# Stick-breaking mask added on VectorE instead of two GpSimd selects, first loads from two queues, and a planned order with margins for waits

## The chip, the core and the metric

The kernel runs on one core of a Trainium2 chip. A core has five engines that run side by side and meet through semaphores: TensorE (PE in the profile, with its weight loads as PEld), VectorE (DVE), ScalarE (ACT), GpSimd (POOL) and SyncE (SP), which here does nothing but issue DMAs. Each engine takes its instructions strictly in the order of its own queue; an instruction that has to wait holds up everything behind it. The metric is the device time of one launch in microseconds (us), the median of three runs.

## The reference

One decoder layer over 512 tokens and a width of 1024, all in fp32. The normalised input is multiplied by one wide input matrix, its columns feed four groups of four heads (64 wide) that mix in four ways, and every group's output is gated, concatenated and multiplied by the output matrix.

```python
def hybrid_layer(x, norm_gain, w_in, b_forget, fox_qk_gain, moba_qk_gain, swa_qk_gain, sinks, w_out, rel_bias):
    hn = rms_norm(x, norm_gain)
    proj = jnp.einsum('btd,de->bte', hn, w_in)
    (fq, fk, fv, ff, fg, mq, mk, mv, mg, sq, sk, sv, sg, wq, wk, wv, wg) = split_columns(proj)
...
    y = jnp.concatenate([from_heads(o_fox) * jax.nn.silu(fg),
                         from_heads(o_moba) * jax.nn.silu(mg),
                         from_heads(o_sb) * jax.nn.silu(sg),
                         from_heads(o_swa) * jax.nn.silu(wg)], axis=-1)
    return x + jnp.einsum('bte,ed->btd', y, w_out)
```

The change touches the arithmetic of one group alone, the stick-breaking heads, called `s` in the kernel (the others are `f`, `m` and `w`):

```python
        z = jnp.einsum('bhqd,bhkd->bhqk', q_i, k).astype(jnp.float32) * ATTN_SCALE
        strict = pos[None, :] < t[:, None]
        log_keep = jnp.where(strict, jax.nn.log_sigmoid(-z), 0.0)
        suffix = lax.cumsum(log_keep, axis=3, reverse=True) - log_keep
        a = jnp.where(strict, jnp.exp(jax.nn.log_sigmoid(z) + suffix), 0.0)
        return jnp.einsum('bhqk,bhkd->bhqd', a.astype(v.dtype), v)
```

The kernel reverses the token order on the host, so that a query block sees itself and the blocks behind it, and the reversed sum over keys becomes a running sum from the left.

## The kernel before

Every fp32 operand of a large product is split into a high part (written by ACT, `hi_copy`, line 134) and a low part (the difference, written by DVE in `lo_part`, lines 139 to 142, or for weight chunks named in `POOL_LO` by GpSimd at line 250). A product is then three matmuls, high by high, high by low, low by high (`mm3`, lines 336 to 338). A 512-wide one starts about 0.23 us after the one before.

Weights come in chunks of up to 512 KB into three raw buffers (`raw`, filled by `load_raw`, line 214), in the order `sv`, `sqk`, `fvf`, `fqk`, `fg`, `sg`, `mqk`, `mv`, `mg`, `wg`, `wqkv`, `o`. A chunk is split into `wh` and `wl`; its raw buffer is then free for the chunk three places later.

The program begins with matmuls of zeros (`warm`, line 156), then loads x transposed (`xT`, eight slices), the first weights (`sv`, two chunks of four loads each) and the small vectors in the order of the string `LOADS` (lines 263 to 272), all of them from SP. ACT loads its table first (line 145). x in its natural layout comes in eight loads (line 769) in the order of `NORMS`; `x_norm` (line 295) makes of two of them the factors `rx` of 128 tokens. When all four are there, `r_row` (line 318) transposes them on PE (tile `rT`), copies them out (`rt`) and sends them through DRAM to all partitions (`rrow`). Line 778 multiplies the `sqk` projections with `rrow`, from which queries and keys of the `s` heads are split (`qs_s`, `k`).

A stick-breaking head (`sb_head`, line 560) does four blocks i of 128 queries against 512, 384, 256 and 128 keys. Per block: scores on PE (lines 505 and 506, or 501 for the last block, tile `s_s`, two PSUM banks in turn), three functions on ACT (lines 577 to 579), a maximum and a sum on DVE (580), a select on GpSimd that zeroes the masked corner (581), the running sum on DVE (583), a difference on DVE (584), a second select on GpSimd that puts -1e30 into the corner (585) and an exponential on ACT (587). The results are transposed on PE (`pT_s`, line 518), copied out in two parts (`pth`, `ptl`) and multiplied with the values (`o_s`, lines 468 and 469). In a tile's name s_s23 is head 2, block 3.

Attention of one group runs among the projections of the next: after each projection step `attend` (line 784) lets the heads go forward by `RATE` units, and by `OUTU` units beside the first half of the output product. The written order is not the final one: `order_engines` (line 1097) reads all instructions, and `_plan` (line 1028) simulates them with costs and latencies written in the program and gives every engine a fixed order. `TURN` moves groups of instructions forward or back in priority, and `PATIENCE` lets an engine wait a little for one of higher priority.

## Time and profile before

| what | value |
|---|---|
| median of 3 runs | 295.74 us (294.53 to 296.07) |
| the profiled execution | 296.93 us |
| its span, first to last instruction | 295.2 us |
| DVE busy | 220.4 us (75%) |
| ACT busy | 194.6 us (66%) |
| GpSimd busy | 116.1 us (39%) |
| bytes moved by DMA | 33.65 MB, mean 114 GB/s |
| granted TensorE clock, mean | 0.994 |

Busy time is the union of an engine's instructions. Matmuls overlap in the array, and their ends are modelled, so an idle stretch of PE in the profile is really idle, while a pause of some 0.1 us between two matmuls does not show. "PEclk" is the TensorE clock that was granted, as a share of full speed. In a row of the timeline stand start, duration, engine, line, operation, tiles and shapes, and in brackets the idle time before it with the one that ended it.

### The profile page before, as it was taken

How to read it: one execution, taken by the hardware profiler on the slowest of the kernel's cores; microseconds unless marked ns; L12 is line 12 of the kernel's file. 1: busy time of each engine (PE TensorE's matmuls, PEld its weight loads, DVE VectorE, ACT ScalarE, POOL GpSimd, SP SyncE). 2: the span in 40 equal slices, each digit the busy share in tenths (PEclk: the TensorE clock that was granted, in tenths of full speed). 3: DMA queues.
4: the chain of work that ended last, by engine and by line, in shares of the span. 5: the costliest groups of instructions: out<-in, count | busy, mean ns of one | idle time of the engine just before them, and what ended most of it. 6: DMA issues, size and time to landing. Idle time of an engine off the chain costs nothing.

```text
span 295.2 us, 4695 instructions
## 1 busy us (share of the span) xinstructions
PE 283.5 (96%) x1529; PEld 236.0 (80%) x1529; DVE 220.4 (75%) x584; ACT 194.6 (66%) x445; POOL 116.1 (39%) x194
## 2 busy tenths in 40 slices
PE   8998999999997899999997999999999999999995
PEld 8987889888885688877876997788888868888884
DVE  1868287969889873699999626896579668999353
ACT  4866089986798653398784447966897839676200
POOL 4505204854157784566426022203440698001010
PEclk9999999999999799999999999999999999999999
DMA  6993606060134059731205412331400345400024
GB/s 194 342 394 124 197 3 188 26 205 18 64 80 136 1 180 263 188 121 37 45 29 149 137 50 92 110 107 30 132 1 18 107 146 192 163 3 0 2 107 178
DMA packets 19960, 33.65 MB, mean 114 GB/s; under 512 B 1616, under 2 KB 10068, under 8 KB 19808
## 3 DMA queue, kind: packets, MB, share of 16 engines
q1 hardware_dynamic: 19936, 33.35, 36.2%
q8 instruction: 12, 0.20, 0.3%
q14 instruction: 12, 0.10, 0.1%
HBM read 31.22 MB, written 4.22 MB: 120 GB/s over the span
## 4 chain that ended last, share of the span: by engine, by line
PE 64%; DVE 13%; ACT 11%; DMA 8%; issue 2%; SPq 1%; POOL 1%; POOLq 0%; DVEq 0%; ACTq 0%
PE o L338 4%; PE o L337 4%; PE o L336 4%; DMA xT<-in_xT 3%; DMA raw_sqk<-in_w_in 3%; PE p_wqkv L336 3%; PE p_wqkv L337 3%; PE p_wqkv L338 3%; PE p_sqk L336 2%; PE p_sqk L338 2%; PE p_sqk L337 2%; ACT k L134 2%; PE pT_m L518 1%; PE pT_f L518 1%; DMA fbc<-sd 1%
## 5 line engine op out<-in xcount | busy, mean ns | idle before, releaser
L250 POOL TENSOR_TENSOR wl_wqkv<-raw_wqkv,wh_wqkv 128x260 fp32r<-128x260 f32 (+1 forms) x12 | 8.5, 737 | 35.9 <-ACT wh_wqkv L134 35.9
L250 POOL TENSOR_TENSOR wl_fqk<-raw_fqk,wh_fqk 128x260 fp32r<-128x260 f32 (+1 forms) x12 | 9.6, 817 | 14.8 <-PE s_s L506 14.1
L583 DVE TENSOR_TENSOR_SCAN pm_s<-l 128x512 f32<-128x512 f32 (+3 forms) x16 | 14.3, 891 | 0.5 <-POOL l L581 0.5
L250 POOL TENSOR_TENSOR wl_o<-raw_o,wh_o 128x260 fp32r<-128x260 f32 (+1 forms) x12 | 9.0, 780 | 14.3 <-issue 14.3
L487 POOL TENSOR_TENSOR oc_w<-oc_w,gate_w 128x512 f32<-128x512 f32 x2 | 2.6, 1285 | 28.3 <-DVE oc_w L482 28.3
L336 PE MATMUL p_sqk<-xh,wh_sqk 128*128 128x512 f32 x32 | 12.6, 400 | 1.0 <-ACT wh_sqk L134 1.0
L585 POOL TENSOR_SCALAR_AFFINE_SELECT pm_s<-pm_s 128x128 f32<-128x128 f32 x16 | 8.9, 556 | 11.2 <-DVE pm_s L584 9.3
L669 POOL TENSOR_SCALAR fxb<-fbc,scol 128x512 f32<-128x512 f32 (+3 forms) x16 | 9.1, 572 | 10.5 <-DMA fbc<-sd 5.2
L336 PE MATMUL p_mqk<-wh_mqk,xh 128*128 128x512 f32 x32 | 13.1, 408 | 0.0
L338 PE MATMUL p_mqk<-wh_mqk,xl 128*128 128x512 f32 x32 | 12.9, 402 | 0.0
L336 PE MATMUL p_wqkv<-wh_wqkv,xh 128*128 128x512 f32 x32 | 12.9, 402 | 0.0
L337 PE MATMUL p_wqkv<-wl_wqkv,xh 128*128 128x512 f32 x32 | 12.8, 401 | 0.0
L336 PE MATMUL p_fqk<-wh_fqk,xh 128*128 128x512 f32 x32 | 12.8, 405 | 0.0
L337 PE MATMUL p_mqk<-wl_mqk,xh 128*128 128x512 f32 x32 | 12.8, 399 | 0.0
L337 PE MATMUL p_fqk<-wl_fqk,xh 128*128 128x512 f32 x32 | 12.8, 399 | 0.0
L338 PE MATMUL p_fqk<-wh_fqk,xl 128*128 128x512 f32 x32 | 12.7, 397 | 0.0
L338 PE MATMUL p_wqkv<-wh_wqkv,xl 128*128 128x512 f32 x32 | 12.6, 395 | 0.0
L139 DVE TENSOR_TENSOR ptl_s<-pT_s,pth_s 128x384 fp32r<-128x384 f32 (+3 forms) x16 | 7.4, 484 | 6.7 <-ACT pth_s L134 6.7
L337 PE MATMUL p_sqk<-xl,wh_sqk 128*128 128x512 f32 x32 | 12.3, 391 | 0.0
L338 PE MATMUL p_sqk<-xh,wl_sqk 128*128 128x512 f32 x32 | 11.7, 390 | 0.0
L581 POOL TENSOR_SCALAR_AFFINE_SELECT l<-l 128x128 f32<-128x128 f32 x16 | 6.9, 433 | 11.5 <-DVE l L580 10.1
L518 PE MATMUL pT_s<-ident,pm_s 128*128 128x128 f32 x40 | 7.9, 279 | 2.9 <-ACT pm_s L587 2.8
(353 smaller groups left out, 1134.6 us busy)
## 6 DMA issues: line engine op xcount, KB each, us to landing
raw_o<-in_w_out SPq DMA_DIRECT2D x8, 512.0 KB, 3.3
xT<-in_xT SPq DMA_DIRECT2D x8, 256.0 KB, 4.1
raw_sqk<-in_w_in SPq DMA_DIRECT2D x4, 512.0 KB, 6.9
x<-in_x SPq DMA_DIRECT2D x8, 256.0 KB, 7.2
raw_fqk<-in_w_in SPq DMA_DIRECT2D x4, 512.0 KB, 3.7
raw_mqk<-in_w_in SPq DMA_DIRECT2D x4, 512.0 KB, 3.7
raw_wqkv<-in_w_in SPq DMA_DIRECT2D x4, 512.0 KB, 3.5
xr<-in_x SPq DMA_DIRECT2D x4, 512.0 KB, 3.5
```

The costliest lines, as they stand in the source:

```text
L134: nc.scalar.activation(dst, src, AF.Copy if isinstance(scale, float) else AF.Identity, scale=scale)
L139: nc.vector.tensor_tensor(dst, src, hi.bitcast(F32), op=ALU.subtract)
L250: nc.gpsimd.tensor_tensor(lv[q], rv[q], hv[q].bitcast(F32), op=ALU.subtract)
L336: nc.tensor.matmul(dst, ah, bh, start=first, stop=False)
L337: nc.tensor.matmul(dst, ah, bl, start=False, stop=False)
L338: nc.tensor.matmul(dst, al, bh, start=False, stop=last)
L487: nc.gpsimd.tensor_tensor(oc, oc, gates[e], op=ALU.mult)
L518: nc.tensor.transpose(pt[:, a * P:(a + 1) * P], pm[:, o:o + P], ident)
L581: nc.gpsimd.affine_select(l[:, :P], l[:, :P], pattern=[[1, P]], base=-1, channel_multiplier=-1, compare_op=ALU.is_ge, fill=0.0)
L583: nc.vector.tensor_tensor_scan(seg, l, l, 0.0, ALU.add, ALU.bypass)
L585: nc.gpsimd.affine_select(seg[:, :P], seg[:, :P], pattern=[[1, P]], base=-1, channel_multiplier=-1, compare_op=ALU.is_ge, fill=NEG)
L669: nc.gpsimd.tensor_scalar(b, bc[:, i * P:], -1.0, scol[:, i, h:h + 1], op0=ALU.mult, op1=ALU.add)
```

## The change

The two GpSimd selects of each stick-breaking block go. In their place a 128x128 tile `smask` (zero, and -1e30 where masked) is made once, and DVE adds it to the masked corner of the scores before ACT reads them, in PSUM in place (for the last block of a head in SBUF). The three functions and the maximum then give zero there by themselves.

The first three loads of `sv` are issued by ACT, ahead of its table load, and `LOADS` has another order. The natural x of tokens 256 to 511 (`HELD`, loads 4 to 7) is planned behind the weight load last issued. Six chunks leave `POOL_LO` (20, 27, 28, 30, 33, 35: one of `mqk`, three of `wqkv`, two of `o`), so that DVE makes their low parts. `RATE` and `OUTU` are smaller, `TURN` has other numbers, and the planner counts a DMA slower and 500 ns later and adds a margin to each wait of PE and ACT on another engine.

```diff
-LOADS = "w0 x0 s x1 w1 x2 w2 x3 w4 w3 x4 x5 w5 x6 w6 w7 x7 q"
-NORMS = "a 0 1 2 3 4 5 6 7 a a a a"
+LOADS = "w0 x0 w1 s w2 x1 x2 x3 w3 x4 w4 x5 w5 x6 w6 x7 w7 q"
+NORMS = "a 0 1 2 3 4 5 a 6 7 a a a"
+BY_ACT, HELD = "w0 w1 w2", {4, 5, 6, 7}
-RATE, OUTU = 5.5, 1.6
+RATE, OUTU = 4.54, 0.55
-POOL_LO = {1, 4, 6, 9, 10, 12, 15, 16, 17, 19, 20, 21, 23, 24, 27, 28, 30, 33, 34, 35, 36, 37,
-           38}
+POOL_LO = {1, 4, 6, 9, 10, 12, 15, 16, 17, 19, 21, 23, 24, 34, 36, 37, 38}
...
-PATIENCE = {"Pool": 10}
+PATIENCE = {"Pool": 10, "PE": 54}
+MARGIN = {"PE": 100, "Activation": 41}
...
-            first[k // 4][k % 4]()
+            first[k // 4][k % 4](nc.scalar if n in BY_ACT.split() else nc.sync)
...
+        if n == BY_ACT.split()[-1]:
+            nc.scalar.preload_act_table_set("natural_log_exp_and_others")
...
+    smask = sb.tile([P, 512], F32, tag="band", name="smask", bufs=2)[:, :P]
+    nc.gpsimd.memset(smask, 0.0)
+    nc.gpsimd.affine_select(smask, smask, pattern=[[1, P]], base=-1, channel_multiplier=-1,
+                            compare_op=ALU.is_ge, fill=NEG)
...
+            nc.vector.tensor_tensor(z[:, :P], z[:, :P], smask, op=ALU.add)
+
             nc.scalar.activation(l, z, AF.Abs)
             nc.scalar.activation(l, l, AF.Exp, scale=-1.0)
             nc.scalar.activation(l, l, AF.Ln, bias=one)
             nc.vector.scalar_tensor_tensor(l, z, 0.0, l, op0=ALU.max, op1=ALU.add)
-            nc.gpsimd.affine_select(l[:, :P], l[:, :P], pattern=[[1, P]], base=-1,
-                                    channel_multiplier=-1, compare_op=ALU.is_ge, fill=0.0)
             nc.vector.tensor_tensor_scan(seg, l, l, 0.0, ALU.add, ALU.bypass)
             nc.vector.tensor_tensor(seg, z, seg, op=ALU.subtract)
-            nc.gpsimd.affine_select(seg[:, :P], seg[:, :P], pattern=[[1, P]], base=-1,
-                                    channel_multiplier=-1, compare_op=ALU.is_ge, fill=NEG)
             nc.scalar.activation(seg, seg, AF.Exp)
...
-            nc.sync.dma_start(xn[t][h], x[t * P:(t + 1) * P, h * 512:(h + 1) * 512])
+            with behind_loads() if int(n) in HELD else nullcontext():
+                nc.sync.dma_start(xn[t][h], x[t * P:(t + 1) * P, h * 512:(h + 1) * 512])
...
-                queue = max(t + 1130, queue) + big * 4 / 360.0
+                queue = max(t + 1130, queue) + big * 4 / 335.0
                 rings.append(queue)
-            src, end = "DMA", queue
+            src, end = "DMA", queue + 500
...
+                if wait and src != e:
+                    d += margin.get(e, 0)
```

The start on ScalarE, before: its first six instructions, where raw_sv is a first weight, wh_sv its high part, xT a slice of x transposed and xh its scaled high part.

```order
L145 ACT_TABLE_LOAD
L134 ACTIVATE wh_sv0_155<-raw_sv0_108 128x256
L134 ACTIVATE xh0_131<-xT0_92,small_70 128x512
L134 ACTIVATE xh0_131<-xT1_93,small_70 128x512
L134 ACTIVATE wh_sv0_155<-raw_sv0_108 128x256
L134 ACTIVATE xh0_131<-xT2_94,small_70 128x512
```

ScalarE at the start, after the change.

```order
L216 DMA raw_sv0_107<-in_w_in 128x256 x3
L276 ACT_TABLE_LOAD
L137 ACTIVATE wh_sv0_160<-raw_sv0_107 128x256 x2
L137 ACTIVATE xh0_131<-xT0_91,small_69 128x512
L137 ACTIVATE wh_sv0_160<-raw_sv0_107 128x256
L137 ACTIVATE xh0_131<-xT1_92,small_69 128x512
L137 ACTIVATE xh0_131<-xT2_93,small_69 128x512
```

Three weight loads now stand ahead of the table load, and two weight splits ahead of the first slice of x.

SyncE's queue from the first `sqk` chunk on, before: x00 to x31 are the eight loads of natural x, two for each 128 tokens.

```order
L214 DMA raw_sqk0_110<-in_w_in 128x2x512
L769 DMA x00_100<-in_x 128x512
L769 DMA x01_101<-in_x 128x512
L769 DMA x10_102<-in_x 128x512
L769 DMA x11_103<-in_x 128x512
L769 DMA x20_104<-in_x 128x512
L769 DMA x21_105<-in_x 128x512
L214 DMA raw_sqk1_221<-in_w_in 128x2x512
L769 DMA x30_106<-in_x 128x512
L769 DMA x31_107<-in_x 128x512
L214 DMA raw_sqk2_289<-in_w_in 128x2x512
L214 DMA raw_sqk3_367<-in_w_in 128x2x512
```

SyncE at the same place, after the change.

```order
L216 DMA raw_sqk0_109<-in_w_in 128x2x512
L777 DMA x00_99<-in_x 128x512
L777 DMA x01_100<-in_x 128x512
L777 DMA x10_101<-in_x 128x512
L777 DMA x11_102<-in_x 128x512
L216 DMA raw_sqk1_226<-in_w_in 128x2x512
L216 DMA raw_sqk2_294<-in_w_in 128x2x512
L777 DMA x20_103<-in_x 128x512
L777 DMA x21_104<-in_x 128x512
L216 DMA raw_sqk3_354<-in_w_in 128x2x512
L777 DMA x30_105<-in_x 128x512
L777 DMA x31_106<-in_x 128x512
```

The second and third `sqk` chunk moved ahead of x20, and the last loads of x behind all four chunks.

PE before, around the last transposition of head 2 (pT_s23; its input pm_s2 is the last of the rows of s_s23): p_fg1 is the second projection step of a gate. From s_s23 to this row stand 12 projection matmuls.

```order
L337 MATMUL p_fg1_1377<-xl0_133,wh_fg0_798 128x512
L338 MATMUL p_fg1_1377<-xh0_131,wl_fg0_799 128x512
L336 MATMUL p_fg1_1377<-xh0_131,wh_fg0_798 128x512
L337 MATMUL p_fg1_1377<-xl0_133,wh_fg0_798 128x512
L518 MATMUL pT_s23_1105<-ident_83,pm_s2_1003 128x128
L338 MATMUL p_fg1_1377<-xh0_131,wl_fg0_799 128x512
```

PE at the same transposition, after the change; p_sg0 is the first step of the next gate.

```order
L342 MATMUL p_sg0_1364<-xh0_131,wl_sg0_1083 128x512
L340 MATMUL p_sg0_1364<-xh0_131,wh_sg0_1082 128x512
L341 MATMUL p_sg0_1364<-xl0_133,wh_sg0_1082 128x512
L522 MATMUL pT_s23_1147<-ident_82,pm_s2_1024 128x128
L342 MATMUL p_sg0_1364<-xh0_131,wl_sg0_1083 128x512
L340 MATMUL p_sg0_1364<-xh0_131,wh_sg0_1082 128x512
```

The transposition stands later by 28 projection matmuls: from s_s23 to it there are now 40 (8 of fg0, 24 of fg1, 8 of sg0).

DVE before, the rows that end with the difference of block s_s23 (l_23 is its work tile, ruf and r0f belong to a query norm).

```order
L741 TENSOR_TENSOR gate_f0_1342<-p_fg0_1317,rrow_135 128x512
L368 TENSOR_REDUCE qms_f3_1196<-sq_f3_1194 128x8
L282 SCALAR_TENSOR_TENSOR ruf2_1081<-r0f2_1079 128x8
L580 SCALAR_TENSOR_TENSOR l_23_1091<-l_23_1091 128x128
L139 TENSOR_TENSOR ptl_s22_1119<-pT_s22_1114,pth_s22_1118 128x384
L283 TENSOR_TENSOR ruf2_1081<-ruf2_1081,rmf2_1080 128x8
L279 TENSOR_SCALAR rmf3_1199<-qms_f3_1196,ex_130 128x8
L583 SCALAR_TENSOR_TENSOR pm_s2_1003<-l_23_1091 128x128
L287 SCALAR_TENSOR_TENSOR r0f2_1079<-ruf2_1081,r0f2_1079 128x8
L580 SCALAR_TENSOR_TENSOR l_30_1225<-s_s30_1222,l_30_1225 128x512
L374 TENSOR_TENSOR nat_f2_1074<-p_fqk2_1049,r0f2_1079 128x512
L584 TENSOR_TENSOR pm_s2_1003<-l_23_1091,pm_s2_1003 128x128
```

DVE after the change, the rows that end with the same difference.

```order
L593 TENSOR_TENSOR pm_s2_1024<-s_s22_1049,pm_s2_1024 128x256
L286 SCALAR_TENSOR_TENSOR ruf3_1126<-r0f3_1124 128x8
L586 TENSOR_TENSOR s_s30_1243<-s_s30_1243,smask_146 128x128
L287 TENSOR_TENSOR ruf3_1126<-ruf3_1126,rmf3_1125 128x8
L591 SCALAR_TENSOR_TENSOR l_23_1136<-l_23_1136 128x128
L291 SCALAR_TENSOR_TENSOR r0f3_1124<-ruf3_1126,r0f3_1124 128x8
L586 TENSOR_TENSOR s_s31_1255<-s_s31_1255,smask_146 128x128
L378 TENSOR_TENSOR nat_f3_1119<-p_fqk3_1061,r0f3_1124 128x512
L142 TENSOR_TENSOR ptl_s22_1161<-pT_s22_1156,pth_s22_1160 128x384
L592 SCALAR_TENSOR_TENSOR pm_s2_1024<-l_23_1136 128x128
L142 TENSOR_TENSOR wl_mqk1_1295<-raw_mqk1_1095,wh_mqk1_1294 128x1024
L593 TENSOR_TENSOR pm_s2_1024<-l_23_1136,pm_s2_1024 128x128
```

The mask additions of head 3 (L586) now stand between the steps of head 2, and a weight split (wl_mqk1) stands ahead of the last difference, which no GpSimd select follows any more.

More of the change, by code (lines that the diff above doesn't have):

```diff
@@ L1 @@
-from contextlib import ExitStack, contextmanager
+from contextlib import ExitStack, contextmanager, nullcontext
 import numpy as np
@@ L47 @@
 OCUT, WARM, WARM_GAPS = 2, 3, 8
-TURN = {"xn": 450, "gate": 10, "qk": -170, "v": -95, "s": -20, "pt": -460, "ot": 210,
-        "gap": 100000, "y": 15, "fb": 100, "w": 95, "pv": 30, "oc": 170, "nat": -10}
-PATIENCE = {"Pool": 10}
+TURN = {"xn": 207, "gate": 18, "qk": -250, "v": -71, "s": 14, "pt": -313, "ot": 134, "gap":
+        100000, "y": 10, "fb": 5, "w": 108, "pv": 16, "oc": 186, "nat": 0, "proj": 61, "x": -110}
+PATIENCE = {"Pool": 10, "PE": 54}
+MARGIN = {"PE": 100, "Activation": 41}
 BOUNDS = list(range(17)) + [21, 27, 35, 46, 59, 77, 99, 128, 166, 216, 280, 363, 470]
@@ L142, in lo_part @@
                                            op1=ALU.subtract)
-    nc.scalar.preload_act_table_set("natural_log_exp_and_others")
     sm_in = cp.tile([P, 22], F32, tag="small", name="small")
@@ L213, in load_raw @@
         raws[s.name, c] = rv
-        return [lambda a=slice(a0, a0 + ka // cut): nc.sync.dma_start(rv[:, a], src[:, a])
+        return [lambda q=nc.sync, a=slice(a0, a0 + ka // cut): q.dma_start(rv[:, a], src[:, a])
                 for a0 in range(0, ka, ka // cut)]
@@ L1025, in _steps, with _plan @@
     return steps
-def _plan(steps, moved, held_back, turn, patience):
+def _plan(steps, moved, held_back, turn, patience, margin):
     at = {s.ins.name: s.k for s in steps}
@@ L1073, in _plan @@
             if s.eng == "Pool":
-                queue = max(t + 1680, queue) + big * 4 / 360.0
+                queue = max(t + 1680, queue) + big * 4 / 335.0
             else:
@@ L1099, in order_engines @@
     last = {}
-    for s, _, _ in _plan(_steps(tc.nc, slots), moved, held_back, TURN, PATIENCE):
+    for s, _, _ in _plan(_steps(tc.nc, slots), moved, held_back, TURN, PATIENCE,
+                         MARGIN):
         if s.eng in last:
```

## The prediction, made before the run

> **What bounds the kernel now.** I read the busy times first, then stretches of the span with the busy time of each engine, then PE's waits.
>
> ```profile
> PE 283.5 (96%) x1529; PEld 236.0 (80%) x1529; DVE 220.4 (75%) x584; ACT 194.6 (66%) x445; POOL 116.1 (39%) x194
> ```
>
> PE is idle for 295.20 - 283.52 = 11.68 us, and the change neither removes nor adds a product, so only idle time, a lowered clock and pauses too short to be listed can be won. Where they lie:
>
> ```profile
> core 0: us, PE busy (x) PEld busy (x) DVE busy (x) ACT busy (x) POOL busy (x), PEclk, DMA share, GB/s
> ...
> 5.02:18.00 12.98, 12.35 (x98) 11.95 (x98) 9.01 (x14) 9.23 (x19) 4.10 (x4) 1.00 1.01 347
> 18.00:30.00 12.00, 11.01 (x50) 8.78 (x49) 9.03 (x34) 7.67 (x19) 4.26 (x5) 1.00 0.60 213
> ...
> 46.00:82.00 36.00, 35.43 (x204) 30.51 (x203) 30.67 (x63) 30.06 (x69) 18.34 (x29) 1.00 0.34 103
> 82.00:97.00 15.00, 12.36 (x58) 9.05 (x56) 12.89 (x29) 12.51 (x29) 9.98 (x21) 1.00 0.36 106
> 97.00:103.00 6.00, 5.74 (x22) 4.73 (x23) 5.22 (x9) 4.54 (x10) 5.23 (x17) 0.72 0.01 1
> 103.00:146.00 43.00, 42.87 (x223) 34.01 (x222) 32.30 (x89) 28.48 (x65) 25.87 (x50) 1.00 0.49 142
> 146.00:161.00 15.00, 13.27 (x76) 10.70 (x76) 14.83 (x46) 9.96 (x27) 7.04 (x10) 1.00 0.26 61
> ...
> 240.00:250.00 10.00, 9.58 (x50) 7.47 (x49) 8.09 (x21) 7.32 (x15) 9.32 (x15) 1.00 0.57 181
> ...
> 290.00:295.20 5.20, 1.90 (x15) 1.61 (x13) 1.54 (x3) 0.00 (x0) 0.00 (x0) 1.00 0.41 152
> ```
>
> The second number is PE's busy time, the one before DMA's share the granted clock. The last row holds 5.20 - 1.90 = 3.30 us behind the last product, which the change leaves as it is. PE's gaps are 0.63 us in the first row, then 0.99, 0.57, 2.64, 0.26, 0.13, 1.73 and 0.42. In 97 to 103 the clock was 0.72, which costs another 6.00 x 0.28 = 1.68 us. What PE waited for:
>
> ```profile
> PE pT_s L518 <- ACT pm_s L587: 2.8, 2, 2.7
> PE p_sqk L336 <- ACT wh_sqk L134: 1.0, 1, 1.0
> PE o_f L469 <- DVE ptl_f L139: 1.0, 1, 1.0
> ```
>
> The reader is to see that one wait, 2.7 us for a stick-breaking block, is by far the largest, and that the lowered clock follows it directly.
>
> **The largest wait.** The timeline of that block, s_s23, from its scores to the transposition:
>
> ```profile
> 89.50 0.39 PE L501 MATMUL s_s<-k,qs_s 128*128 128x256 f32 x1
> ...
> 92.57 0.29 DVE L580 SCALAR_TENSOR_TENSOR l<-l 128x128 f32<-128x128 f32 x1
> ...
> 93.00 0.29 POOL L581 TENSOR_SCALAR_AFFINE_SELECT l<-l 128x128 f32<-128x128 f32 x1 [0.25 <-DVE l L580]
> ...
> 96.23 0.27 DVE L584 TENSOR_TENSOR pm_s<-l,pm_s 128x128 f32<-128x128 f32 x1
> ...
> 96.58 0.29 POOL L585 TENSOR_SCALAR_AFFINE_SELECT pm_s<-pm_s 128x128 f32<-128x128 f32 x1 [0.44 <-DVE ruf L282]
> ...
> 97.26 0.33 PE L518 MATMUL pT_s<-ident,pm_s 128*128 128x128 f32 x1 [2.67 <-ACT pm_s L587]
> ```
>
> The block needs 97.26 - 89.50 = 7.76 us, and PE had only twelve projection matmuls and the scores of the next head to put in between. The two selects sit on this chain: 93.00 + 0.29 - 92.86 = 0.43 us for the first and 96.87 - 96.50 = 0.37 us for the second. Removing them alone takes 0.8 us of 7.76, so the selects are not what the wait is made of; their place in the order is. These rows give the pitch of PE:
>
> ```profile
> 87.31 0.39 PE L338 MATMUL p_fg<-xh,wl_fg 128*128 128x512 f32 x1
> 87.54 0.40 PE L336 MATMUL p_fg<-xh,wh_fg 128*128 128x512 f32 x1
> ```
>
> At 0.23 us each, the 40 projections that now stand there cover 9.2 us, and with two score pairs and six transpositions about 10.7 us. Against that stand 7.76 - 0.8, the mask addition, and a 1.2 us weight split ahead of the last difference: about 8.5 us. PE is covered by 2 us. I take the idle time of 82 to 97 and the clock loss, 2.64 + 1.68 = 4.3, less 0.2 that stays: **-4.1**. Bounds: -4.5, and 0 if another block inherits the wait with its clock loss.
>
> The row of 97 to 103 shows the clock falling after 2.67 us of idleness, while the 0.99 us of 18 to 30 left it at 1.00. The Trainium skill ("TensorE: Matmul & The Clock Gate", "Why this matters for your kernels") puts the limit at idle gaps of about 3 us. By that rule the wait would have cost no clock, this term would be -2.4, and the forecast 291.7; here the trace is below that limit and the clock fell, so I go by the trace.
>
> **The opening.** First ACT and the zeros:
>
> ```profile
> 0.79 1.28 ACT L145 ACT_TABLE_LOAD   x1 [0.79 <-PEq L1124]
> ...
> 0.84 4.61 PE L156 MATMUL warm<-const-float32-0.0 128*128 128x128 f32 x20 [0.84 <-PEq L1124]
> ...
> 1.70 0.43 SPq L272 DMA_DIRECT2D small<-in_small  x1
> ...
> 4.17 0.72 ACT L134 ACTIVATE xh<-xT,small 128x512 fp32r<-128x512 f32 x1 [0.76 <-DMA small<-in_small]
> ...
> 5.10 0.56 PE L336 MATMUL p_sv<-wh_sv,xh 128*128 128x256 f32 x1
> ...
> 6.48 0.72 ACT L134 ACTIVATE xh<-xT,small 128x512 fp32r<-128x512 f32 x1 [1.60 <-DMA xT<-in_xT]
> ```
>
> Ten zero matmuls are 20 passes; the first product came at 5.10, so a pass takes 0.213 us. All eleven now stand first, and PE is free at 0.84 + 22 x 0.213 = 5.5; the filler that stood later (0.43 us) goes, so that is even. ACT issues three loads (0.46 us from one issue to the next), loads its table from 2.2 to 3.5, splits two weights (some 0.7) and scales the first x from 4.1 to 4.9; the small vectors, issued 0.46 earlier, land 2.5 us after their issue, at 3.7. The first product is ready before the zeros end. PE then has 12 products of 0.12 us, until 7.0. The second slice of x was the fourth issue and is now the third, with the weights on another queue; half a microsecond earlier puts xh at 6.0 to 6.7. I take 0.63 of idle time down to 0.2.
>
> The table load moves from idle time into ACT's path. Whether more than the load itself must pass is seen in the middle of the run:
>
> ```profile
> 208.65 1.28 ACT L747 ACT_TABLE_LOAD   x1
> 209.95 1.15 ACT L747 ACTIVATE gate_f<-gate_f 128x512 f32<-128x512 f32 x2
> ```
>
> The next activation starts 0.02 us behind it. The Trainium skill ("ScalarE: Activation LUTs", "What ACT_TABLE_LOAD costs") adds a drain of about 1.38 us to each switch. By it the first x would be ready at about 6.3 instead of 4.9, some 0.9 us behind the zeros, and the sum would be 0.9 smaller; no drain stands in these rows, so I count none.
>
> Next the `sqk` weights and the moved x:
>
> ```profile
> 22.03 1.06 ACT L134 ACTIVATE wh_sqk<-raw_sqk 128x1024 fp32r<-128x1024 f32 x1 [0.43 <-DMA raw_sqk<-in_w_in]
> ...
> 24.86 0.68 DVE L300 CUSTOM_DVE_ANT_0 xj<-x 128x512 f32<-128x512 f32 x1
> ...
> 37.41 1.89 DVE L778 TENSOR_TENSOR sqk<-p_sqk,rrow 128x512 f32<-128x512 f32 x3 [5.22 <-DMA rrow<-rxd]
> ```
>
> The second chunk has two x loads of 256 KB fewer ahead; at the 347 GB/s of the row above that is 0.76 us each, 1.5 us in all, more than the 0.99 of PE's gap. The last x load has two more 512 KB chunks ahead, at most 3.0 us. It hides behind the 12.5 us from its square (24.86) to the use of rrow (37.41); if that cover is gone, the scores start later, and PE's `fvf` products fill in. I take 0.99 down to 0.2, which makes the opening **-1.2**; bounds -1.6 and +1.0.
>
> **The other gaps.** In 146 to 161 DVE is busy for 14.83 of 15.00 us: it is the bound there, and the three waits add to 1.73. With `RATE` at 4.54 instead of 5.5 the same heads spread over a fifth more projection work, but one weight split of `mqk` comes to DVE. I take half, **-0.9**; bounds 0 and -1.7. The gap of 46 to 82 is a wait for a score bank that a select helped to hold: **-0.3** of 0.57. Of the 0.42 and 0.13, **-0.2**.
>
> **What the change adds.**
>
> ```profile
> L573 DVE TENSOR_TENSOR l<-s_s,l x4: 255/274/292, 58.5 to 107.2; 128x128 f32<-128x128 f32 x4
> ...
> L139 DVE TENSOR_TENSOR wl_wg<-raw_wg,wh_wg 128x1024 fp32r<-128x1024 f32 x2 | 2.5, 1225 | 2.3 <-ACT wh_wg L134 2.3
> ...
> L250 POOL TENSOR_TENSOR wl_wqkv<-raw_wqkv,wh_wqkv 128x260 fp32r<-128x260 f32 (+1 forms) x12 | 8.5, 737 | 35.9 <-ACT wh_wqkv L134 35.9
> ...
> L585 POOL TENSOR_SCALAR_AFFINE_SELECT pm_s<-pm_s 128x128 f32<-128x128 f32 x16 | 8.9, 556 | 11.2 <-DVE pm_s L584 9.3
> ...
> L581 POOL TENSOR_SCALAR_AFFINE_SELECT l<-l 128x128 f32<-128x128 f32 x16 | 6.9, 433 | 11.5 <-DVE l L580 10.1
> ```
>
> The nearest row to a mask addition is a 128x128 sum out of PSUM, 0.274 us; 16 are 4.4 us. Six weight splits at 1.225 are 7.3 us. DVE goes from 220.4 to about 232 us, four fifths of the span. GpSimd loses 6.9 + 8.9 for the selects and 6 x 4 x 0.737 = 17.7 for the splits, and goes from 116.1 to about 83. All this lies beside PE as long as the chains have cover. The addition puts DVE's queue ahead of ACT's first function: behind the waiting function stand copies that PE needs. Ends: 0, and 16 x (0.274 + one split of 1.225) = 24 if every block shows in full. A table of other numbers makes waits of its own somewhere; before, apart from the largest, a wait was 0.3 to 1.0 us. I take **+1.0**, near the row of the hidden additions. Pauses below 0.15 us do not show; ten would be up to 1.5, kept for the range as -1.5.
>
> **Sum.** -4.1 - 1.2 - 0.9 - 0.3 - 0.2 + 1.0 = -5.7. The profiled execution took 296.93 us (span 295.20, 1.73 around it) and would take 291.2; the median of the runs stands 1.2 lower, and 295.74 - 5.7 = **290.0**.
>
> **Rivals.** (1) The waits move instead of going. DVE, full in 146 to 161, stays the bound there with the added split, so that nothing of the 0.9 is won, and two new waits of 1.0 come where the `w` heads now run later, beside the output product. For it: DVE at 14.83 of 15.00. Against: slower pace of the heads. -5.7 + 0.9 + 2.0 = -2.8, **293.0**; chance 0.22. (2) Slower: the mask addition waits in DVE's queue behind one wide instruction, ACT behind it, and PE runs out of cover in each of the 16 blocks. It decides from 7.2 / 16 = 0.45 us shown per block; at 0.75 us (the addition and half a scan) it is +12, **302**. For it: DVE at 12.89 of 15 in 82 to 97. Against: 2 us of cover at the worst block. Chance 0.12. (3) It does not do what it says: PE at 96% never waited for the selects, the early loads are bound by the DMA engines (share 1.01 from 5 to 18), and another block inherits the largest wait. What is left is **295**; chance 0.09.
>
> **Chances.** The forecast has 0.57. A measurement of this kernel can tell about 0.5%, 1.5 us, from no change. Faster are forecast and rival 1: 0.79; the same is rival 3: 0.09; slower rival 2: 0.12. The best bounds give -1.6 - 4.5 - 1.7 - 0.57 - 0.55 - 1.5 = -10.4, or 285.3, and the range reaches up to rival 3: **285 to 295**, with rival 2 left out.
>
> **What would show it.** Right: in the profile after, PEclk 1.00 in every slice, no PE wait above 1.2 us, PE idle below 8 us, the wait for wh_sqk gone, DVE near 232 us, GpSimd near 83. Wrong: a PE wait of 2 us or more with a lowered clock behind it; the first products waiting for ACT; PE waiting for pT_s or s_s behind a mask addition; scores of head 0 later than now.

## The result and the profile after

The changed kernel takes 290.69 us (median of four runs, 290.25 to 291.27) against 295.13 for the kernel before in the same comparison (294.38 to 296.07). The ratio is 0.9849, with a 95% interval of 0.981 to 0.9888. The profiled execution took 290.52 us, its span 288.7.

The busy times, and the granted clock in the 40 slices:

```profile
PE 280.4 (97%) x1529; PEld 235.9 (82%) x1529; DVE 233.6 (81%) x606; ACT 193.8 (67%) x445; POOL 89.5 (31%) x140
...
PEclk9999999999999999999999999999999999999999
```

Stretches of the span after the change, with the same columns as the stretches in the prediction:

```profile
5.50:18.00 12.50, 12.04 (x97) 11.63 (x97) 9.61 (x17) 9.78 (x22) 4.60 (x4) 1.00 1.01 349
18.00:30.00 12.00, 12.00 (x55) 9.95 (x55) 10.12 (x28) 6.51 (x13) 6.15 (x7) 1.00 0.74 244
30.00:46.00 16.00, 14.85 (x80) 12.48 (x79) 10.22 (x19) 9.43 (x15) 4.21 (x5) 1.00 0.42 123
46.00:82.00 36.00, 35.50 (x203) 30.28 (x202) 32.28 (x77) 28.77 (x69) 7.54 (x8) 1.00 0.23 70
82.00:97.00 15.00, 14.41 (x72) 11.68 (x71) 13.16 (x29) 11.49 (x26) 11.19 (x24) 1.00 0.36 107
97.00:103.00 6.00, 5.64 (x26) 4.30 (x25) 6.00 (x8) 4.02 (x8) 3.70 (x8) 1.00 0.52 168
103.00:146.00 43.00, 42.65 (x223) 34.14 (x222) 35.16 (x94) 30.12 (x70) 17.14 (x33) 1.00 0.43 118
146.00:161.00 15.00, 14.76 (x110) 13.68 (x109) 14.94 (x49) 10.16 (x27) 8.41 (x15) 1.00 0.45 124
...
238.00:250.00 12.00, 11.37 (x60) 8.66 (x59) 11.71 (x39) 7.87 (x25) 4.63 (x7) 1.00 0.46 143
```

What PE waited for (total, times, longest):

```profile
PE pT_s L522 <- ACT pm_s L594: 0.9, 2, 0.6
...
PE s_s L510 <- DVE k L142: 0.7, 1, 0.7
PE o L342 <- DVE yl_m L142: 0.6, 1, 0.6
...
PE s_s L509 <- ACT k L137: 0.4, 1, 0.4
```

The reader is to see four things. The wait of 2.7 us and the lowered clock behind it are gone: PE's gap between 82 and 103 fell from 2.90 us to 0.59 + 0.36. The f heads' stretch, 146 to 161, lost nearly all of its gap (1.73 to 0.24). The opening, 5 to 46, has as much idle time as before: the gap of 0.99 before 30 is gone, and a new one of 1.15 stands at the first scores. PE's idle time fell from 11.7 to 288.7 - 280.4 = 8.3, by 3.3 before rounding, and its busy time by 3.1 at an equal number of matmuls. Of these the clock explains 1.7; the other 1.4 I take for pauses too short to be listed, which no row shows.

From profile to profile the gain is 6.4 us, in medians 4.4. The kernel before has the lowered clock in only some of its executions: of 51 more that ran beside the experiments, 29 had a mean clock of 0.994 or less and a median of 295.87, and 22 had 0.998 or more and a median of 294.62. The one in the prediction (0.994, 296.93) paid for it.

### The profile page after: what moved, and what is told of

The parts are those of the page before. It is cut to its first block, busy times and chain, and to the rows that moved or that the text cites. A ratio compares the mean times of both kernels' runs of the same rounds, so it can differ in the third digit from the quotient of the medians.

```text
span 288.7 us, 4641 instructions
## 1 busy us (share of the span) xinstructions
PE 280.4 (97%) x1529; PEld 235.9 (82%) x1529; DVE 233.6 (81%) x606; ACT 193.8 (67%) x445; POOL 89.5 (31%) x140
## 4 chain that ended last, share of the span: by engine, by line
PE 68%; DVE 20%; ACT 8%; DMA 2%; issue 1%; ACTq 0%
PE o L342 5%; PE o L341 5%; PE o L340 4%; DVE pm_s L592 3%; PE p_wqkv L342 3%; PE p_wqkv L341 3%; PE p_wqkv L340 3%; PE p_sqk L341 2%; PE p_sqk L340 2%; PE p_sqk L342 2%; PE p_fqk L341 2%; PE p_fqk L340 2%; PE p_fqk L342 2%; DMA raw_sv<-in_w_in 2%; PE pT_m L522 2%; DVE pm_f L548 1%
## 5 line engine op out<-in xcount | busy, mean ns | idle before, releaser
L252 POOL TENSOR_TENSOR wl_fqk<-raw_fqk,wh_fqk 128x260 fp32r<-128x260 f32 (+1 forms) x12 | 11.8, 1010 | 18.9 <-ACT wh_fqk L137 18.9
L491 POOL TENSOR_TENSOR oc_f<-oc_f,gate_f 128x512 f32<-128x512 f32 x2 | 2.6, 1297 | 43.1 <-ACT gate_f L754 43.1
L676 POOL TENSOR_SCALAR fxb<-fbc,scol 128x512 f32<-128x512 f32 (+3 forms) x16 | 10.4, 654 | 17.4 <-DVE qs_f L144 10.4
L592 DVE TENSOR_TENSOR_SCAN pm_s<-l 128x512 f32<-128x512 f32 (+3 forms) x16 | 15.0, 942 | 0.1
L252 POOL TENSOR_TENSOR wl_sg<-raw_sg,wh_sg 128x256 fp32r<-128x256 f32 x8 | 7.0, 914 | 25.0 <-ACT wh_sg L137 25.0
L142 DVE TENSOR_TENSOR ptl_m<-pT_m,pth_m 128x384 fp32r<-128x384 f32 (+3 forms) x16 | 7.3, 484 | 4.1 <-ACT pth_m L137 4.1
L137 ACT ACTIVATE pth_m<-pT_m 128x384 fp32r<-128x384 f32 (+3 forms) x16 | 6.5, 435 | 5.6 <-PE pT_m L522 5.4
L594 ACT ACTIVATE pm_s<-pm_s 128x512 f32<-128x512 f32 (+3 forms) x16 | 7.3, 465 | 4.1 <-DVE pm_s L593 3.9
```

Of the source, the lines that this page charges most:

```text
L137: nc.scalar.activation(dst, src, AF.Copy if isinstance(scale, float) else AF.Identity, scale=scale)
L142: nc.vector.tensor_tensor(dst, src, hi.bitcast(F32), op=ALU.subtract)
L252: nc.gpsimd.tensor_tensor(lv[q], rv[q], hv[q].bitcast(F32), op=ALU.subtract)
L491: nc.gpsimd.tensor_tensor(oc, oc, gates[e], op=ALU.mult)
L592: nc.vector.tensor_tensor_scan(seg, l, l, 0.0, ALU.add, ALU.bypass)
L594: nc.scalar.activation(seg, seg, AF.Exp)
```

## Experiments

Where a part of the change is taken out or put in, the planner orders the whole program anew, so such a run shows the part with an order of its own. Four runs keep the order of their base and move, or add, named rows only. Each ratio is against the kernel before, run beside it. A difference from the changed kernel compares medians of different rounds of runs; the kernel before had medians of 295.13 to 295.54 in them, so a few tenths of such a difference say nothing.

### One row of PE moved

The theory after the first look was that of the prediction: the place of one row, the last transposition of s_s23, makes the largest wait. In the kernel before, with its order kept:

```diff
+MOVES = [('PE', 'pth_s23', 9), ('PE', 'pT_s23', 10)]
...
+    plan = [s for s, _, _ in _plan(_steps(tc.nc, slots), moved, held_back, TURN, PATIENCE)]
+    for e, out, by in MOVES:
+        q = [s for s in plan if s.eng == e]
+        i = max(j for j, s in enumerate(q) if any(a.name.startswith(out) for a in s.reads + s.writes))
+        q.insert(i + by, q.pop(i))
...
```

> The kernel before with its order kept, and one row of PE moved: the last transposition of s_s23 stands ten rows later (behind eight more projection matmuls and one score pair, 8 x 0.23 + 0.5 = 2.3 us), and the first product with its copy nine rows later. Nothing else differs: selects, opening, tables and planner are those of before. Theory (the place of this row in the order made the wait, and the clock loss followed from it): the wait of 2.67 us falls to about 0.4, the clock is 1.00 in every slice, and the time falls by 2.3 + 1.7 = 4.0, to about 291. Rival (the wait is made by the length of the chain with its selects and moves to the next row that needs this block): a new wait of 2 us at pT_s21 or o_s, time within 1 us of before. Rival (the clock loss has nothing to do with the wait): 293.

Measured: 298.72 us, ratio 1.0112 (1.0079 to 1.0146), slower. PE's waits in this run, and then rows of its VectorE:

```profile
PE s_s L505 <- DVE pm_s L584: 3.9, 2, 3.5
PE pT_s L518 <- DVE ptl_s L139: 1.2, 1, 1.2
```

```profile
95.36 0.27 DVE L584 TENSOR_TENSOR pm_s<-l,pm_s 128x128 f32<-128x128 f32 x1
...
96.13 1.22 DVE L583 TENSOR_TENSOR_SCAN pm_s<-l 128x512 f32<-128x512 f32 x1
...
97.85 0.68 DVE L584 TENSOR_TENSOR pm_s<-s_s,pm_s 128x512 f32<-128x512 f32 x1
```

The transposition no longer waits. The next row that needs VectorE does, the scores of head 3: their PSUM bank comes free with the difference at 97.85, and PE waited 3.50 us for it, with the lowered clock behind (mean 0.992). My theory and the two rivals of the expectation all missed this row, but the first rival had the kind right: the wait moved. The 1.2 us at a later pT_s come behind the copies of the late transposition, so I take them for a consequence of the move itself. What fills VectorE's queue here, from 87.7 to 98.5 with one break of 0.57 us, is the work of the s heads and, nearly as much, the query norms and a gate of the f heads; the transposition was only where PE met it first.

### One part alone, on the kernel before

The mask alone:

```diff
...
+            nc.vector.tensor_tensor(z[:, :P], z[:, :P], smask, op=ALU.add)
...
-            nc.gpsimd.affine_select(l[:, :P], l[:, :P], pattern=[[1, P]], base=-1,
...
-            nc.gpsimd.affine_select(seg[:, :P], seg[:, :P], pattern=[[1, P]], base=-1,
...
```

> Before with the mask addition in place of the selects; old opening, old tables, old planner. The planner orders everything anew, and by its order 26 projection matmuls now stand between s_s23 and its last transposition (12 before). Theory (the order counts, not the selects): 14 x 0.23 = 3.2 us more cover, the largest wait below 0.5, clock 1.00, and since nothing else is better about 291 to 292; the gaps of 5 to 30 and of 146 to 161 stay as they were. Rival (the selects themselves were the price): the same or better, 290.5, and the two runs without the mask stay at 294 to 295. Rival (an addition on VectorE costs in every block): 300 or more.

Measured: 304.24, ratio 1.0303 (1.0275 to 1.0332). PE's waits:

```profile
PE s_f L505 <- DVE nm_f L544: 4.7, 1, 4.7
PE pT_s L518 <- ACT pm_s L590: 4.3, 2, 3.8
```

The cover that I counted in the order, 26 projections instead of 12, did not help: the wait at the s heads grew to 3.8, and a second one of 4.7 came at the first scores of the f heads. That is near the rival which let the addition cost in every block, but the loss is in these waits and the clock behind them, not spread over 16 blocks.

The opening alone (`LOADS`, `NORMS`, `BY_ACT` and `HELD` as changed, the table load behind the third load):

```diff
-LOADS = "w0 x0 s x1 w1 x2 w2 x3 w4 w3 x4 x5 w5 x6 w6 w7 x7 q"
...
+LOADS = "w0 x0 w1 s w2 x1 x2 x3 w3 x4 w4 x5 w5 x6 w6 x7 w7 q"
...
+BY_ACT, HELD = "w0 w1 w2", {4, 5, 6, 7}
...
```

> Before with the new opening alone (three loads issued by ScalarE ahead of its table load, the new order of loads, the last loads of x planned behind the weights); selects, tables and planner as before. Ordered anew; 24 projection matmuls stand between s_s23 and its last transposition. Theory: the wait for wh_sqk goes (1.0), the scores of head 0 come no earlier since they wait for rrow, so the opening keeps some 0.4 of it; the largest wait falls by 12 x 0.23 = 2.7 us, with the clock at 1.00: 291 to 292 in all. Rival (the mask or the tables are needed for the largest wait): wait of over 2 us stays, 294 to 295. Rival (the opening is worth its 1.2 in full): 1.2 less at the first score of head 0.

Measured: 294.32 (ten runs, 293.19 to 296.35), ratio 0.9969 (0.9938 to 0.9999). The waits for pT_s were 1.2 and 0.6 and the clock 1.00 in every slice, as the theory had it; the time is 2 to 3 us above its number, and barely below the kernel before: waits came elsewhere (1.3 at s_f, 1.0 at qT_w).

The tables and the planner alone (`RATE`, `OUTU`, `POOL_LO`, `TURN`, `PATIENCE`, `MARGIN`, DMA costs):

```diff
-RATE, OUTU = 5.5, 1.6
+RATE, OUTU = 4.54, 0.55
...
+MARGIN = {"PE": 100, "Activation": 41}
...
+            src, end = "DMA", queue + 500
...
```

> Before with the new tables and planner alone (RATE and OUTU, the six weight splits on VectorE, TURN, PATIENCE, the margins and the slower DMA of the planner); selects and opening as before. 30 projection matmuls stand between s_s23 and its last transposition. Theory (the tables carry most): largest wait below 0.5, clock 1.00, the f heads' waits of 146 to 161 lower by 1 to 2, about 290.5 to 291.5. Rival (the mask is needed): 294 or more, with waits for pT_s behind the selects. Rival (the six splits on VectorE cost): VectorE above 230 us busy and new waits of PE for low parts, 293.

Measured: 293.40, ratio 0.9928 (0.9901 to 0.9955). The wait of the s heads is gone without the mask; instead the stretch of 143 to 154 waits four times (0.38, 0.83, 0.69, 0.96), with a lowered clock behind the last. So the mask is not needed for the largest wait, and the number is that of the last rival, though VectorE's busy time stayed a little below the 230 us that it named (229.5). Of the changed kernel's 4.4 us this is about half.

### One part undone, in the changed kernel

The old pace:

```diff
-RATE, OUTU = 4.54, 0.55
+RATE, OUTU = 5.5, 1.6
```

> The changed kernel with RATE and OUTU of before (5.5 and 1.6) and all else as changed; ordered anew, 13 projection matmuls stand between s_s23 and its last transposition (40 in the changed kernel). Theory now (VectorE is the bound of the s heads: in the run with one row moved it worked without a break from 87.7 to 98.5 while PE waited, so only a slower pace of the heads removes the wait): the wait returns, 2 to 5 us with a lowered clock behind it, and the f heads of the next stretch wait more as well: 296 to 302. Rival (TURN, margins and planner carry the gain, the pace does nothing): within 1 us of 290.7. Rival (the opening and the mask carry it): the same, within 1 us.

Measured: 296.46, ratio 1.0041 (1.0019 to 1.0062): 5.8 us slower than the changed kernel. PE's waits, close together between 90.9 and 96.3, with VectorE named in each and two halved stretches of the clock behind them (mean 0.988):

```profile
PE s_s L505 <- DVE pm_s L593: 1.5, 1, 1.5
PE s_s L509 <- DVE l L582: 1.1, 1, 1.1
PE s_s L509 <- DVE pm_s L593: 0.9, 2, 0.5
```

The theory holds for the s heads; that the f heads wait more was wrong, none of their waits is listed.

The selects back on GpSimd:

```diff
-            nc.vector.tensor_tensor(z[:, :P], z[:, :P], smask, op=ALU.add)
+            nc.gpsimd.affine_select(l[:, :P], l[:, :P], pattern=[[1, P]], base=-1,
+                                    channel_multiplier=-1, compare_op=ALU.is_ge, fill=0.0)
...
+            nc.gpsimd.affine_select(seg[:, :P], seg[:, :P], pattern=[[1, P]], base=-1,
+                                    channel_multiplier=-1, compare_op=ALU.is_ge, fill=NEG)
```

> The changed kernel with the two selects on GpSimd instead of the mask addition, all else as changed; ordered anew. Tables alone gave 293.4 with old opening and selects, the opening alone 1.2 less than before. Theory (with the slower pace the mask is worth little, since the selects are off the bound: chains have room): 291 to 292.3. Rival (the mask carries the 1.5 that opening and tables by themselves leave unexplained): 292.2 or more, with waits of PE for pT_s behind the selects. Rival (the addition on VectorE costs 16 x 0.3): 288 to 289.

Measured: 291.96, ratio 0.9892 (0.9853 to 0.993), which overlaps with the changed kernel's interval. With the other parts in place the medians differ by 1.3 us, which the intervals do not tell from nothing. This run has no wait for pT_s at all, but one of 2.28 us of p_fg for a query norm on VectorE.

The old opening:

```diff
-BY_ACT, HELD = "w0 w1 w2", {4, 5, 6, 7}
+BY_ACT, HELD = "", set()
```

with `LOADS`, `NORMS` and the place of the table load as before.

> The changed kernel with the opening of before (all loads from SyncE, table load first, old order of loads, no load held back), mask and tables as changed; ordered anew. Theory (the opening's gain at the first products is mostly lost again at the first scores): 291 to 292, and the wait for wh_sqk of 1 us is there again. Rival (the opening is worth its 1.2 and more): 292 to 293. Rival (nothing): 290.7.

Measured: 292.69, ratio 0.9923 (0.9894 to 0.9953): 2.0 us slower, the first rival's number. The wait for wh_sqk is there again (1.2), and by the new order also 1.7 and 1.3 at the s heads, so that not all of the 2.0 is the opening's.

### The rows that lost the opening's gain

Rows of VectorE, GpSimd and PE in the timeline of the changed kernel (wl_fvf are low parts of the next weights):

```profile
36.80 0.97 DVE L142 TENSOR_TENSOR wl_fvf<-raw_fvf,wh_fvf 128x780 fp32r<-128x780 f32 x1 [4.34 <-ACT wh_fvf L137]
37.94 0.70 DVE L142 TENSOR_TENSOR wl_fvf<-raw_fvf,wh_fvf 128x520 fp32r<-128x520 f32 x1 [0.17 <-ACT wh_fvf L137]
38.55 1.88 DVE L786 TENSOR_TENSOR sqk<-p_sqk,rrow 128x512 f32<-128x512 f32 x3
...
39.82 4.21 POOL L252 TENSOR_TENSOR wl_fqk<-raw_fqk,wh_fqk 128x260 fp32r<-128x260 f32 x4 [10.79 <-ACT wh_fqk L137]
...
40.47 4.11 DVE L144 SCALAR_TENSOR_TENSOR qs_s<-sqk,qs_s 64x512 fp32r<-64x512 f32 x4
...
43.59 0.68 PE L509 MATMUL s_s<-k,qs_s 128*128 128x512 f32 x2 [0.44 <-ACT k L137]
45.34 0.68 PE L510 MATMUL s_s<-k,qs_s 128*128 128x512 f32 x2 [0.71 <-DVE k L142]
```

Two things hold up the first scores. VectorE waits for wh_fvf, does two low parts, and only then takes up rrow, which before stood at the head of its queue. And the four low parts of the queries take 4.11 us beside GpSimd's wl_fqk; before they took 2.84. Three rows moved, the order else kept:

```diff
+MOVES = [('DVE', 'wl_fvf2', 3), ('DVE', 'wl_fvf1', 3), ('Activation', 'wh_fqk0', 8)]
```

> The changed kernel with its order kept but for three rows: on VectorE the two low parts wl_fvf stand behind the three multiplications with rrow instead of ahead of them, and on ScalarE the high part wh_fqk stands behind the queries and keys of the first s heads instead of ahead of them (so GpSimd's low parts of fqk start later too, away from the low parts of the queries, which took 1.10 us beside them and 0.68 without). Theory (these rows lost the opening's gain, 0.44 + 0.71 us of waits at the first scores): both waits go, and about 1.1 is won: 289.5. Rival (rrow's arrival alone decides when the scores can start): the waits stay within 0.3 and the time within 0.4 of 290.7. Rival (PE now waits for wl_fvf or wl_fqk): new waits at p_fvf or p_fqk, slower.

Measured: 289.03 (288.32 to 289.35), ratio 0.9781 (0.9753 to 0.9809). The rows of this run:

```profile
36.31 1.89 DVE L786 TENSOR_TENSOR sqk<-p_sqk,rrow 128x512 f32<-128x512 f32 x3 [4.53 <-DMA rrow<-rxd]
38.12 1.57 DVE L142 TENSOR_TENSOR wl_fvf<-raw_fvf,wh_fvf 128x780 fp32r<-128x780 f32 x2
39.72 2.84 DVE L144 SCALAR_TENSOR_TENSOR qs_s<-sqk,qs_s 64x512 fp32r<-64x512 f32 x4
...
42.57 0.57 PE L509 MATMUL s_s<-k,qs_s 128*128 128x512 f32 x2
...
43.76 6.64 POOL L252 TENSOR_TENSOR wl_fqk<-raw_fqk,wh_fqk 128x260 fp32r<-128x260 f32 x8 [15.41 <-ACT wh_fqk L137]
```

Both waits are gone, the low parts of the queries take 0.71 us each again, and the scores start 1.0 us earlier. All four runs lie below the fastest of the changed kernel, so in these runs this version beats both. Of the 1.7 us between the medians the two waits explain 1.15; the last experiment, which has these rows too, took 288.5 to 291.1, so how much of the 1.7 holds is open.

### Every mask addition twice

The order of the changed kernel kept, and a second addition behind each:

```diff
+            EXTRA[nc.vector.tensor_tensor(z[:, :P], z[:, :P], smask, op=ALU.add).ins.name] = one_add.ins.name
```

> The changed kernel with every mask addition done twice, the second right behind the first on VectorE, and no other row of any engine moved (16 more instructions of about 0.28 us, 4.5 us of VectorE; masked scores become -2e30 instead of -1e30, which gives the same zeros). It prices one more addition on the chain of each block. Rival 2 of the prediction (each addition shows): between 16 x 0.28 = 4.5 (all show) and 12 us slower than the changed kernel, 295 to 302. Theory (nearly all of it lies beside PE, but where VectorE is full, in 82 to 103, a few show): 0.5 to 1.5 slower, 291 to 292, the waits of s_s23's transposition longer by about twice 0.28. Rival (hidden altogether): 290.7 within 0.3.

Measured: 292.68 (nine runs, 291.36 to 295.41), ratio 0.9924 (0.9895 to 0.9953): 2.0 us slower than the changed kernel, a little above the theory's range. The profiled execution was the slowest of the nine (295.41, with 0.8 us more at wh_sqk and 0.9 at the first products); its waits:

```profile
PE pT_s L523 <- ACT pm_s L596: 2.5, 3, 1.3
...
PE p_fqk L342 <- DVE wl_fqk L143: 0.5, 1, 0.5
```

The waits for pT_s grew from 0.9 to 2.5, and 0.5 came at p_fqk: 2.1 us, about what the medians show. In this order, an addition shows 2.0 / 16 = 0.12 us per block, not the 0.45 from which rival 2 would decide.

### Pace alone, and no margins

The new `RATE` and `OUTU` alone on the kernel before (the diff is that of the old pace, reversed):

> Before with RATE and OUTU of the changed kernel alone (4.54 and 0.55); selects, opening, TURN, splits and planner as before. 28 projection matmuls stand between s_s23 and its last transposition (12 before). Theory (the pace removes the largest wait): no wait of PE over 1.5 us in 80 to 105, clock 1.00 there, 292 to 293.5, as the run with all the tables (293.4). Rival (pace needs the other tables): 295 or slower, with waits elsewhere. Rival (the pace explains the changed kernel by itself): 291.

Measured: 301.49, ratio 1.0211 (1.018 to 1.0242). The waits:

```profile
PE s_s L505 <- DVE pm_s L584: 3.1, 2, 2.5
PE pT_m L518 <- DVE pm_m L552: 2.8, 4, 1.2
PE p_mv L336 <- DVE nat_m L374: 1.5, 1, 1.5
```

The theory of the pace falls as a cause by itself: the wait for VectorE at the s heads stays, and the m heads and a projection wait for VectorE as well.

The changed kernel without margins and with the old DMA costs in the planner:

```diff
-MARGIN = {"PE": 100, "Activation": 41}
+MARGIN = {}
...
-                queue = max(t + 1130, queue) + big * 4 / 335.0
+                queue = max(t + 1130, queue) + big * 4 / 360.0
...
-            src, end = "DMA", queue + 500
+            src, end = "DMA", queue
```

> The changed kernel with a planner that adds no margin to waits and counts DMAs as before; mask, opening, pace, splits and TURN as changed; ordered anew. Theory (margins matter little, the pace carries the tables' part): 290 to 292. Rival (margins are what makes the order hold on the chip): several new waits of 0.5 to 1 us, 293 or more.

Measured: 296.20, ratio 1.0032 (1.0008 to 1.0056): 5.5 us slower than the changed kernel, and no faster than the kernel before. Its waits, and the stretch of the f heads:

```profile
PE pT_f L522 <- DVE pm_f L556: 1.8, 3, 1.0
...
PE p_fvf L341 <- DVE wl_fvf L142: 0.8, 1, 0.8
```

```profile
146.00:161.00 15.00, 13.16 (x90) 11.64 (x90) 13.18 (x35) 9.03 (x23) 8.26 (x12) 1.00 0.41 123
```

The rival was right. The clock is 1.00 throughout, and the wait of the s heads is no larger (1.0 in all); the f heads' gap of 146 to 161 is back at 1.84 us, from 0.24, with 90 matmuls in it instead of 110. Of the 5.5 us another 2.5 is PE's busy time (282.9 instead of 280.4 for as many matmuls), which I take for pauses too short for the list. Margins and DMA costs were put back together; which of the two it is was not tried apart.

### The remaining short waits

The run with the `sqk` rows moved, and eleven more rows of PE:

```diff
+MOVES = [('DVE', 'wl_fvf2', -1, 3), ('DVE', 'wl_fvf1', -1, 3), ('Activation', 'wh_fqk0', 0, 8),
+         ('PE', 's_s02', -1, 2), ('PE', 's_s02', -2, 2), ('PE', 'pT_s23', -1, 2), ('PE', 'pT_s22', -1, 3),
+         ('PE', 'pT_s23', -2, 3), ('PE', 's_f31', -1, -7), ('PE', 'p_mv1', 0, -7), ('PE', 'p_mv1', 1, -7),
+         ('PE', 'p_mv1', 2, -7), ('PE', 'o101', -1, 3), ('PE', 'o100', -1, 3)]
```

> The run with the sqk rows moved (289.0), and on PE eleven rows moved by two to seven places so that rows which are ready stand ahead of the five short waits of that run: s_s02 (0.50), the transpositions of s_s23 at 92.4 (0.56) and 98.3 (0.51), o_f behind ptl_f (0.72), the output products behind yl_m (0.63). Nothing else differs. Theory (a short wait with ready work behind it goes when the row goes; unlike the 2.67 of before, where VectorE was full for 11 us): 0.46, 0.5, 0.46, 0.5 and 0.6 are won, 2.3 to 2.5 less in all, about 286.7. Rival (every wait of PE there stands for an engine that is full, so it comes back at the next row): 288.5 to 289.

Measured: 290.34 (six runs, 288.52 to 291.12), ratio 0.9821 (0.9793 to 0.985). Nothing is won. Its waits:

```profile
PE p_sqk L340 <- ACT wh_sqk L137: 1.2, 1, 1.2
...
PE p_mv L340 <- DVE nat_m L378: 0.7, 1, 0.7
```

The first wait is the opening's, whose rows are the same as in the run that it started from, where this wait is not listed: the second high part of sqk starts on ScalarE at 20.2 here and at 18.4 there, so the start differs from one execution to another. I therefore compare from the first scores on: to the span's end this run takes 288.8 - 44.1 = 244.7 us, and the run that it started from 287.6 - 42.6 = 245.0. In place of the five waits, 2.9 us in all, stand others of 2.2: 0.7 for VectorE at p_mv instead of the one at o_f, 0.4 and 0.2 at pT_s, 0.3 at s_w, and 0.2 each at o_s, at s_s and in the first scores. PE's idle time from the first scores to the last product fell from 3.4 to 2.7 us, its busy time rose by 0.4 at the same 1291 matmuls, and 0.3 us was won. The rival, that these waits stand for an engine that is full and come back at the next row, is the likelier reading; what the 0.4 is made of, no row shows.

| part | alone on the kernel before (295.5) | undone in the changed kernel (290.7) |
|---|---|---|
| mask | 304.2 | 292.0 |
| opening | 294.3 | 292.7 |
| tables and planner | 293.4 | |
| of these, pace | 301.5 | 296.5 |
| of these, margins and DMA costs | | 296.2 |

The parts do not add up. Mask and pace, each alone, make the kernel slower; undone in the changed kernel, four parts cost 1.3 + 2.0 + 5.8 + 5.5 = 14.6 us, over three times what all of them win together. Each of these runs also has an order of its own, so none of these numbers is the price of its part alone.

## Why the prediction was right, and where its steps were not

The time, 290.0, and the range held. Term by term, from profile to profile:

| term | predicted | measured |
|---|---|---|
| largest wait with its clock | -4.1 | -1.95 idle, -1.7 clock |
| opening | -1.2 | -0.1 |
| 146 to 161 | -0.9 | -1.5 |
| 46 to 82 | -0.3 | -0.1 |
| 103 to 146, 161 to 210, 240 to 250 | -0.2 | +0.3 |
| new waits | +1.0 | in the rows above (1.15 at the first scores, 0.6 at yl_m) |
| pauses | 0 | -1.4 |

That the sum came out near is in part luck. The opening gave 1.1 us less than predicted and the largest wait 0.45 less, and this was made up by 0.6 more in 146 to 161 and by the 1.4 of busy time, which the prediction left out of the sum and kept for the range alone. In medians the gain is 4.4 where 5.7 was forecast; 290.0 lies within 0.7 of 290.69 because the kernel before stood at 295.13 in that comparison and not at 295.74.

**The largest wait.** That it goes with its clock loss was right, and its size nearly so. The reason was right in part only. The prediction said that "their place in the order" makes it, and that 40 projections cover the block by 2 us. The 40 do stand there, and PE worked for some 11.1 us between, a little more than the 10.7 that I took. But in the changed kernel the same block takes not 8.5 but 100.14 - 88.11 = 12.0 us:

```profile
88.11 0.28 PE L505 MATMUL s_s<-k,qs_s 128*128 128x256 f32 x1
...
97.87 1.68 DVE L142 TENSOR_TENSOR wl_mqk<-raw_mqk,wh_mqk 128x1024 fp32r<-128x1024 f32 x1
99.47 0.28 DVE L593 TENSOR_TENSOR pm_s<-l,pm_s 128x128 f32<-128x128 f32 x1
...
100.14 0.33 PE L522 MATMUL pT_s<-ident,pm_s 128*128 128x128 f32 x1 [0.36 <-ACT pm_s L594]
```

The cover was used up to 0.36 us below nothing. Cover in the order is not cover in time, since the chain also grows with what stands in VectorE's queue. VectorE did not get less to do in this stretch: between 82 and 103 it is busy for 19.2 us, before for 18.1. What changed is that PE has 40 projections to do meanwhile and not 12. The moved row and the mask alone (26 projections, a wait of 3.8) show that counting rows of PE does not tell this wait; VectorE's queue has to be laid beside it.

**The opening** was the term that failed: -0.1 instead of -1.2. The first product came right behind the zeros, at 5.50, and the wait for wh_sqk went, both as predicted. But "PE's `fvf` products fill in" was the cover that I named, and the scores stand between these products in PE's order: PE came to them 1.15 us too early and could not go on to the rest. What made the scores late for PE is that the low parts of `fvf` had moved ahead of rrow's use on VectorE, and that a GpSimd split stretched the queries' low parts. I had followed the moved loads, and not the rows of VectorE between the loads and the scores. With three rows put back the waits go. In the working of the table load, 6.3 is 0.8 us behind the zeros' end at 5.5, not 0.9; the sum does not use it.

**The f heads** gave more than the half that I took. VectorE is still full there (14.94 of 15.00), as rival 1 said, yet PE does not wait: more matmuls stand in that stretch, 110 instead of 76. The run without margins shows how far this hangs on the planner's margins and DMA costs, of which the prediction said nothing.

**Additions and marks.** PE's idle time is 8.3 where I named less than 8; no wait is above 1.2, as named. Of the signs of being wrong, one came in small: PE waited 0.3 us for ACT at the first products. The scores of head 0 start at 43.59, before at 45.14, and the longest wait for pT_s or s_s is 0.7. Predicted for VectorE and GpSimd were 232 and 83 us, measured are 233.6 and 89.5. Rival 2 falls with the doubled mask. In the mask alone, however, a slower kernel did come, by 8.7 us: its mechanism was two long waits for VectorE and the clock behind them.

**The clock** was counted in full from one execution. Of 51 executions of the kernel before, 29 paid for it, and their median is 1.25 us above that of the others. This is part of why the gain in medians, 4.4, is less than from profile to profile, 6.4: the profiled execution paid, and at 296.93 it was also slower than the median of those that did, 295.87.

Open remain: what the margins of PE and ACT and the DMA costs do apart, what the six splits, `TURN` and `PATIENCE` do by themselves, and whether another set of tables would make the mask worth more than 1.3 us.

## What to carry to other kernels

Where PE is busy for 96% of the time and a planner sets the order, a change is not the sum of its parts: each edit makes a new order, and parts put in alone moved this kernel by -2 to +9 us, with waits at places that the edit did not touch. Here a wait that was moved away on PE came back at the next row that needed the same engine; before predicting that rows moved on PE remove a wait, lay the rows of the engine it waits for beside them. Where an early load is won, follow it to the first product that needs all of its chain, and look at what was put ahead of each step on the way.
